# Half-size products for 14 of the 24 column tiles of a linear-attention in-projection, with the residual stream parked in device memory

## The chip, the cores and the metric

The kernel runs on one NeuronCore of a Trainium2 chip. The metric is the device time of one execution in microseconds (us): the median of three runs before the change is 1865.31 us. One further execution was recorded by the hardware profiler; all rows of the profile come from it.

## The reference, cut to what matters

A two-layer decoder over 512 tokens and 16 prepended meta tokens (528 together), width 1024. Each layer is a half-step SwiGLU FFN, a token mixer, and another half-step FFN, each between two RMS norms. Layer 0's mixer is chunked gated linear attention (GLA); the change touches only its in-projection.

```python
def gla_mixer(hn, w_in, w_gate, b_gate, g_head, w_out):      # hn = rmsnorm(h, g[2]), (1, 528, 1024)
    q, k, v, r, lr = jnp.split(hn @ w_in, [512, 1024, 2048, 3072], axis=-1)
    gk = log_sigmoid(lr @ w_gate + b_gate) / 16.0
    ...                                  # 4 heads, key width 128, value width 256, chunks of 64 tokens
    o = o_intra + einsum('bhncd,bhndv->bhncv', q_dec, states)
    o = rmsnorm(o, g_head) * silu(r)     # per head
    return o.reshape(B, L, 1024) @ w_out
h = h + rmsnorm(mix, g[3])
```

`hn @ w_in` has 24 column tiles of 128: 4 of q (tiles 0 to 3, one per head), 4 of k (4 to 7), 8 of v (8 to 15, two per head), 8 of r (16 to 23), and 16 narrow columns lr for the forget gate.

## The kernel before

Everything is kept transposed: features on the 128 partitions, tokens along the free dimension, so that a matmul takes a 128x128 weight tile as the stationary operand and streams tokens. Each float32 operand is split into a high half (rounded to float32r by ScalarE) and a low half (the rest, by VectorE); a product is three matmuls, high x high, low x high, high x low (`mm3s`, and `product` in `Item`).

**Orders.** The order of TensorE's instructions is that of the program text. A small planner in the program, `Flow`, keeps a clock that each matmul moves on; generators (`right_factors`, `core`, `gates`, `gated` and others) yield delays, and their next instructions are put between matmuls when the clock has come so far. The instructions of the other engines and the DMA queues (SP's, POOL's) are put in an order of their own by the compiler's scheduler when the program is built. Each engine then works through its list in order and waits for semaphores.

**Weights.** `units` is the list of weight loads in order of use; `next_w` and `next_pair` take the next one, `prefetch` loads ahead. A plain tile is two raw 128x512 loads and two splits (`split_part`, L268 and L269 of the profile: ScalarE's copy and VectorE's subtraction). A unit that is a list is a pair of tiles for the seven-product scheme (`split_pair`): five raw loads on SP, two accumulating loads on POOL, seven splits (L284, L285) and two additions (L290).

**The seven-product scheme** exists in the FFNs. Two column tiles and the two halves of the contraction (4 k-tiles of 128 each) form a 2x2 block matrix, the two token halves (264 tokens) the other side. `right_factors` scales H by gain and norm factor R into xs, copies H to device memory (`h_kept`) so that its space is free, and makes seven split operands z ("11", "t1", "22", "t2", "21", "t3", "t4"). `Item` with `head`, `body`, `tail` runs the seven products of 12 matmuls in banks a (two), c (two) and d (one), and the next item's head stands before the current one's tail. `Strassen` allots the banks.

**GLA.** `x_first` multiplies the tiles k0, q0, v0, v1; then for each head a generator `core(h)` is spawned, which does scans of the gate, transposes (pv, pm, pk, pt), scores (pa, pb), states (ps, st), outputs (po, pn) and the head's norm (half_go). Meanwhile `x_units` multiplies the next head's four tiles, each over two token groups of 272 and 256 tokens; `evac` multiplies by R out of PSUM. The last eight tiles are r; `gated` applies tanh and the head's output to each of 16 halves and splits the result into og, and `out_proj` follows. A head's core begins when the gates, its tiles and the middle of the previous core are done.

PSUM has eight banks. SBUF holds 42 slots of 128 x 2 x 528 floats and 13 raw slots of 128x512.

## Time and profile before

| | us |
|---|---|
| median of 3 runs (lowest, highest) | 1865.31 (1865.19, 1866.03) |
| the profiled execution | 1864.76 |
| its span, first to last instruction | 1863.0 |
| PE busy (matmul) | 1841.3 |
| DVE busy (VectorE) | 1449.7 |
| ACT busy (ScalarE) | 1145.6 |
| POOL busy (GpSimd) | 375.7 |
| in-projection tiles (`x_l0m`), first to last matmul | 369.7 to 562.1 |

PE is TensorE's matmuls, PEld its weight loads, DVE VectorE, ACT ScalarE, POOL GpSimd, SP the engine that asks for most DMAs; a q behind a name is that engine's queue of DMA issues. A row of groups gives line, engine, operation, output and inputs, count, busy time, the mean of one, then the idle time before them with what ended it. Lines are those of the kernel before. Consecutive instructions of an engine overlap a little, so the pace is read from start to start.

### The profile page before, as it was taken

The page shows a single profiled execution, that of the slowest core. Times are in us where ns is not written, and L with a number is a line of the kernel's source. Part 1 is how long each engine was busy: PE and PEld are TensorE (multiplying, and loading weights), DVE is VectorE, ACT ScalarE, POOL GpSimd, SP SyncE. Part 2 cuts the span into 40 slices and gives each one's busy share as a digit, 9 for nine tenths or more (in the row PEclk, how much of TensorE's full clock was granted, in tenths as well). Part 3 has the DMA queues.
Part 4 walks back from the last instruction along what each step waited for, and adds up shares of the span by engine and source line. Part 5 has one row for each costly group of instructions (what it writes and reads, how often), then busy time and mean ns, then how long its engine had stood idle before and what let it go on. Part 6 is the DMA issues. An engine that isn't in the chain of part 4 may idle for free.

```text
span 1863.0 us, 39130 instructions
## 1 busy us (share of the span) xinstructions
PE 1841.3 (99%) x14743; PEld 1780.2 (96%) x14743; DVE 1449.7 (78%) x2965; ACT 1145.6 (61%) x2677; POOL 375.7 (20%) x535
## 2 busy tenths in 40 slices
PE   9999999999999999999999999999999999999998
PEld 9999999999999999999999899999988898999998
DVE  6887888767664788787888788888767679889884
ACT  5666666654446566666674566666667756666664
POOL 2111113320001411111333111213320141111232
PEclk9999999999999999999999999999999999999999
DMA  7655769421123365576953565769521235557691
GB/s 248 191 147 154 187 149 275 167 69 58 64 62 114 104 180 140 156 182 158 277 200 103 138 162 154 187 152 270 174 74 52 69 103 163 150 158 185 155 292 49
DMA packets 153357, 282.77 MB, mean 152 GB/s; under 512 B 16848, under 2 KB 45392, under 8 KB 153168
## 3 DMA queue, kind: packets, MB, share of 16 engines
q1 hardware_dynamic: 113056, 194.94, 32.5%
q0 software_dynamic: 39680, 84.75, 22.2%
q8 instruction: 115, 1.88, 0.4%
q14 instruction: 74, 0.61, 0.1%
q10 hardware_dynamic: 432, 0.59, 0.1%
HBM read 235.00 MB, written 44.70 MB: 150 GB/s over the span
## 4 chain that ended last, share of the span: by engine, by line
PE 77%; DVE 12%; ACT 6%; issue 3%; DMA 1%; POOL 1%; DVEq 0%; SPq 0%; ACTq 0%; POOLq 0%
PE a L201 22%; PE x L201 17%; PE y L201 16%; PE c L201 11%; PE d L201 5%; DVE raw L290 3%; ACT w_s L284 2%; DVE w L285 2%; DVE w_s L285 1%; DMA raw<-in_w_in 1%; ACT s L1581 1%; ACT w L284 1%; PE po L201 1%; PE o L201 1%; DVE w L269 1%
## 5 line engine op out<-in xcount | busy, mean ns | idle before, releaser
L285 DVE TENSOR_TENSOR w_s<-raw,w_s 128x512 fp32r<-128x512 f32 (+1 forms) x416 | 267.3, 648 | 114.3 <-ACT w_s L284 110.7
L284 ACT ACTIVATE w_s<-raw 128x512 fp32r<-128x512 f32 (+1 forms) x416 | 244.5, 593 | 161.4 <-DVE raw L290 159.9
L285 DVE TENSOR_TENSOR w<-raw,w 128x512 fp32r<-128x512 f32 (+1 forms) x312 | 199.5, 645 | 6.1 <-ACT w L284 4.0
L290 DVE TENSOR_TENSOR raw<-raw,raw 128x512 f32<-128x512 f32 (+1 forms) x304 | 192.1, 632 | 5.2
L344 POOL DMA_DIRECT2D raw<-in_w_in x112 | 103.0, 943 | 444.9 <-DVE w_s L285 72.0
L269 DVE TENSOR_TENSOR w<-raw,w 128x512 fp32r<-128x512 f32 x248 | 166.2, 700 | 33.4 <-ACT w L268 32.1
L284 ACT ACTIVATE w<-raw 128x512 fp32r<-128x512 f32 (+1 forms) x312 | 181.1, 586 | 0.0
L201 PE MATMUL x<-x_l0m,w 128*128 128x272 f32 (+1 forms) x1152 | 152.2, 289 | 0.0
L201 PEld LDWEIGHTS x<-x_l0m,w 128*128 128x128 f32 x1152 | 143.4, 189 | 2.7 <-issue 1.7
L268 ACT ACTIVATE w<-raw 128x512 fp32r<-128x512 f32 x248 | 143.8, 619 | 0.3
L519 POOL TENSOR_TENSOR acc_post<-acc_post,sq_post 128x256 f32<-128x256 f32 (+1 forms) x77 | 61.5, 799 | 361.0 <-ACT sq_post L518 256.7
L201 PE MATMUL y<-hidl0f,w 128*128 128x272 f32 (+1 forms) x960 | 120.4, 286 | 1.2 <-DVE hidl0f L525 1.0
L201 PEld LDWEIGHTS y<-hidl0f,w 128*128 128x128 f32 x960 | 118.1, 188 | 2.2 <-DVE hidl0f L525 1.6
L201 PE MATMUL a<-zl0f_t,w_s 128*128 128x264 f32 x864 | 119.3, 286 | 0.7 <-DVE w_s L285 0.7
L201 PE MATMUL a<-zl1f_t,w_s 128*128 128x256 f32 x864 | 116.1, 283 | 1.2 <-ACT c L1094 0.6
L201 PE MATMUL y<-hidl1f,w 128*128 128x256 f32 (+1 forms) x768 | 115.2, 310 | 0.4 <-DVE hidl1f L525 0.4
L201 PEld LDWEIGHTS y<-hidl1f,w 128*128 128x128 f32 x768 | 104.9, 188 | 9.3 <-DVE hidl1f L525 0.8
L201 PEld LDWEIGHTS a<-zl0f_t,w_s 128*128 128x128 f32 x864 | 110.3, 188 | 2.8 <-DVE w_s L285 1.6
L201 PEld LDWEIGHTS a<-zl1f_t,w_s 128*128 128x128 f32 x864 | 107.1, 188 | 4.1 <-ACT c L1094 1.9
L201 PE MATMUL x<-x_l0f,w 128*128 128x256 f32 (+1 forms) x768 | 98.6, 287 | 1.5 <-DVE w L269 1.1
L201 PEld LDWEIGHTS x<-x_l0f,w 128*128 128x128 f32 x768 | 95.0, 188 | 3.1 <-DVE w L269 1.9
L201 PE MATMUL x<-x_l1f,w 128*128 128x256 f32 (+1 forms) x576 | 93.3, 320 | 2.1 <-ACT x_l1f L547 1.8
(570 smaller groups left out, 4088.3 us busy)
## 6 DMA issues: line engine op xcount, KB each, us to landing
raw<-in_w_in SPq DMA_DIRECT2D x408, 256.0 KB, 4.1
raw<-in_w_in POOLq DMA_DIRECT2D x112, 256.0 KB, 5.1
raw<-in_w_down SPq DMA_DIRECT2D x128, 192.0 KB, 2.3
raw<-in_w_last SPq DMA_DIRECT2D x48, 256.0 KB, 6.3
raw<-in_gla_in SPq DMA_DIRECT2D x48, 256.0 KB, 3.4
kept_y<-dn POOLq DMA_DIRECT2D x16, 528.0 KB, 7.5
raw<-in_w_out SPq DMA_DIRECT2D x32, 256.0 KB, 3.2
kept_y<-dn POOLq DMA_DIRECT2D x16, 512.0 KB, 8.1
```

The source lines that it names most:

```text
L201: inst = pe.matmul(o, lhs, rhs, start=start, stop=stop, skip_group_check=onto)
L268: act.activation(w[:, 0, :m], raw[:, :m], AF.Copy)
L269: dve.tensor_tensor(w[:, 1, :m], raw[:, :m], w[:, 0, :m].bitcast(F32), op=ALU.subtract)
L284: act.activation(w[:, 0, :m], src, AF.Copy)
L285: dve.tensor_tensor(w[:, 1, :m], src, w[:, 0, :m].bitcast(F32), op=ALU.subtract)
L290: dve.tensor_tensor(dst, dst, src, op=ALU.add)
L344: pool.dma_start(r, src, accum_op=ALU.add)
L519: pool.tensor_tensor(sums[0][:, :n], sums[0][:, :n], t[:, :n], op=ALU.add)
L1581: act.activation(s[:, c], s[:, c], AF.Exp, scale=rc[:, c % 2 : c % 2 + 1], bias=nm[:, c : c + 1], accum_out=den[:, c : c + 1],)
```

## The change

Of the 24 tiles, the first ten in order (k0, q0, v0, v1, k1, q1, v2, v3, k2, q2) stay plain. The other fourteen become seven pairs: (v4, v5), (k3, q3), (v6, v7) and four pairs of r. `right_factors` is spawned after `x_first`; it writes H to device memory, and `bring_back_h`, cut out of the FFN, reads it back at the end of the stage. A new `Projected` item evacuates: since the z operands already hold R, five copies on ACT and two additions on DVE per pair replace the multiplications by R. There is one bank c instead of two. `gated` works on 528 tokens at once instead of two halves. Heads 0 and 1 are begun after plain tiles, core 2 after the first pair, core 3 after the third.

```diff
-GLA_ORDER = [4, 0, 8, 9, 5, 1, 10, 11, 6, 2, 12, 13, 7, 3, 14, 15] + list(range(16, 24))
+GLA_ORDER = [4, 0, 8, 9, 5, 1, 10, 11, 6, 2]
+GLA_PAIRS = [(12, 13), (7, 3), (14, 15), (16, 17), (18, 19), (20, 21), (22, 23)]
...
                 units += [a["gla_in"][u] for u in GLA_ORDER]
+                units += [[a["gla_in"][u] for u in pair] for pair in GLA_PAIRS]
...
+    def bring_back_h(kept):
         H.fresh()
         for q in range(KD // 2):
             rows = slice(2 * q, 2 * q + 2)
             pool.dma_start(H[:, rows, kept], h_kept[:, rows, kept])
...
     class Strassen:
-        def __init__(self, z, halves):
+        def __init__(self, z, halves, banks=2):
...
-            self.a, self.c = tiles.a[i], tiles.c[i]
+            self.a, self.c = tiles.a[i], tiles.c[i % len(tiles.c)]
...
+    class Projected(Item):
+        nk = 4
+
+        def __init__(self, tiles, first, second, scale=1.0):
+            super().__init__(tiles)
+            o, n = tiles.o, self.n
+            self.first, self.second = ([t[:, c : c + n] for c in (o, o + n)] for t in (first, second))
+            self.scale = -scale
+
+        def right(self, name, k):
+            return (self.tiles.z[name][k // 2][:, i, k % 2] for i in range(2))
+
+        def body(self):
+            self.product(self.c, "s1", "t1", True)
+            act.activation(self.second[1], self.c, AF.Copy, scale=self.scale)
+            self.product(self.a, "s2", "t2", False)
+            act.activation(self.first[1], self.a, AF.Copy)
+            self.product(self.d, "12", "21", False)
+            act.activation(self.first[0], self.d, AF.Copy)
+            self.product(self.a, "s3", "t3", False)
+            dve.scalar_tensor_tensor(self.second[1], self.a, self.scale, self.second[1], op0=ALU.mult, op1=ALU.add)
+
+        def tail(self):
+            self.product(self.c, "s4", "22", False)
+            dve.tensor_tensor(self.first[1], self.c, self.first[1], op=ALU.add)
+            self.product(self.a, "22", "t4", False)
+            act.activation(self.second[0], self.a, AF.Copy, scale=self.scale)
+            released[0] += 1
...
-            def gated(m, g, p):
-                o, n = g
-                if rg[m] is None:
-                    rg[m] = duo(f"rg{m}")
-                gs, th = (t[:, o : o + n] for t in rg[m])
-                dve.tensor_tensor(gs, p[:, :n], x.rt[:, o : o + n], op=ALU.mult)
+            def gated(m):
+                gs, th = rg[m]
                 act.activation(th, gs, AF.Tanh, scale=0.5)
                 dve.scalar_tensor_tensor(gs, th, 1.0, gs, op0=ALU.add, op1=ALU.mult)
                 yield cores[m // 2 if m < 4 else 3]
...
-                dve.scalar_tensor_tensor(gs, gs, gn, V[:, m, o : o + n], op0=ALU.mult, op1=ALU.mult)
-                split(og[m], gs, g)
+                dve.scalar_tensor_tensor(gs, gs, gn, V[:, m], op0=ALU.mult, op1=ALU.mult)
+                split(og[m], gs, (0, TOK))
...
-            late = []
-            for h in range(HEADS):
-                cores.append(flow.spawn(core(h, [gate] + late + mids[h - 1 : h])))
-                if h + 1 < HEADS:
-                    kk = [("k", h + 1), ("q", h + 1), ("v", 2 * h + 2), ("v", 2 * h + 3)]
-                    late = x_units(x, 4, L0, lambda i, g, p, kk=kk: evac(*kk[i], g, p))
+            n2 = TOK // 2
+            halves, z, plain = [(0, n2), (n2, n2)], {}, Job(None)
+            factors = flow.spawn(right_factors(x, halves, z, plain))
+
+            def begin_core(h, late):
+                cores.append(flow.spawn(core(h, [gate] + late + mids[max(h - 1, 0) : h])))
+
+            begin_core(0, [])
+            kk = [("k", 1), ("q", 1), ("v", 2), ("v", 3)]
+            begin_core(1, x_units(x, 4, L0, lambda i, g, p: evac(*kk[i], g, p)))
+            late = x_units(x, 2, L0, lambda i, g, p: evac("kq"[i], 2, g, p))
+            plain.finish(flow)
+            flow.wait(factors)
+            set_ahead(16, RING)
+            tiles = Strassen(z, halves, 1)
             jobs = []
-            set_ahead(8)
-            x_units(x, KD, L0, lambda i, g, p: jobs.append(flow.spawn(gated(i, g, p))))
-            flow.wait(*jobs[:12])
+            def values(m):
+                return Projected(tiles, V[:, m], V[:, m + 1])
+
+            def keys():
+                qk[3] = duo("qk3")
+                return Projected(tiles, qk[3][1], qk[3][0], 128 ** -0.5)
+
+            def gating(m):
+                rg[m], rg[m + 1] = duo(f"rg{m}"), duo(f"rg{m + 1}")
+                return Projected(tiles, rg[m][0], rg[m + 1][0])
+
+            def finish_gates(m):
+                jobs.extend([flow.spawn(gated(m)), flow.spawn(gated(m + 1))])
+
+            nothing = lambda: None
+            plan = [(lambda: values(4), lambda: begin_core(2, late)), (keys, nothing), (lambda: values(6), lambda: begin_core(3, []))]
+            plan += [(lambda m=m: gating(m), lambda m=m: finish_gates(m)) for m in range(0, KD, 2)]
...
+            cur = begin(0)
+            for i in range(len(plan)):
+                cur.body()
+                nxt = begin(i + 1)
+                cur.tail()
+                plan[i][1]()
+                cur = nxt
+            bring_back_h(slice(0, TOK))
+            flow.wait(*jobs[:6])
             set_ahead(16)
             cap[0] = used[0] + 12
             out_proj(og, L0, L0, True, finish, 5, jobs=jobs, late=2)
```

More of the change, by code (lines that the diff above doesn't have):

```diff
@@ L927, in ffn @@
                 pool.dma_start(Y[:, rows, right], y_right[:, rows, right], accum_op=ALU.add)
+        bring_back_h(kept)
+        set_ahead(32)
+        cap[0] = min(end, len(units))
+        for _ in proj:
+            pass
+    def bring_back_h(kept):
         H.fresh()
@@ L931, in ffn @@
             pool.dma_start(H[:, rows, kept], h_kept[:, rows, kept])
-        set_ahead(32)
-        cap[0] = min(end, len(units))
-        for _ in proj:
-            pass
     def right_factors(x, halves, z, plain):
@@ L987, in trunk_kernel @@
     class Strassen:
-        def __init__(self, z, halves):
+        def __init__(self, z, halves, banks=2):
             self.z, (self.o, self.n) = z, halves[0]
-            self.a, self.c = ([ps(f"{nm}{used[0]}_{i}")[:, : self.n] for i in range(2)] for nm in "ac")
+            self.a, self.c = ([ps(f"{nm}{used[0]}_{i}")[:, : self.n] for i in range(k)] for nm, k in (("a", 2), ("c", banks)))
             self.d = ps(f"d{used[0]}")[:, : self.n]
@@ L1391, in gated @@
                 yield cores[m // 2 if m < 4 else 3]
-                if og[m] is None:
-                    og[m] = pair_tile(f"og{m}")
+                og[m] = pair_tile(f"og{m}")
                 gn = vec[:, V_GN + m % 2 : V_GN + m % 2 + 1]
-                dve.scalar_tensor_tensor(gs, gs, gn, V[:, m, o : o + n], op0=ALU.mult, op1=ALU.mult)
-                split(og[m], gs, g)
+                dve.scalar_tensor_tensor(gs, gs, gn, V[:, m], op0=ALU.mult, op1=ALU.mult)
+                split(og[m], gs, (0, TOK))
             kinds = [("k", 0), ("q", 0), ("v", 0), ("v", 1)]
@@ new lines, in finish_gates, with begin @@
+            def finish_gates(m):
[3 more added lines that the diff above has]
+            plan += [(lambda m=m: gating(m), lambda m=m: finish_gates(m)) for m in range(0, KD, 2)]
+            def begin(i):
+                if i == len(plan):
+                    return None
+                t = plan[i][0]()
+                t.head()
+                return t
```

## The prediction

> **What bounds the kernel now.** I read the page first (spans, slices, the chain that ended last), then the stage the change touches through the views of windows, timeline, groups and waits.

> ```profile
> span 1863.0 us, 39130 instructions
> ...
> PE 1841.3 (99%) x14743; PEld 1780.2 (96%) x14743; DVE 1449.7 (78%) x2965; ACT 1145.6 (61%) x2677; POOL 375.7 (20%) x535
> ...
> PEclk9999999999999999999999999999999999999999
> ...
> PE 77%; DVE 12%; ACT 6%; issue 3%; DMA 1%; POOL 1%; DVEq 0%; SPq 0%; ACTq 0%; POOLq 0%
> ```

> TensorE is busy 99% of the span at full granted clock and carries 77% of the last chain. A matmul saved is worth its pace, as long as VectorE (78%) keeps delivering. The stage itself, beside two windows of the first FFN, where the same seven-product scheme already runs:

> ```profile
> 399.19:562.23 163.04, 163.04 (x1243) 154.46 (x1239) 106.78 (x256) 75.77 (x184) 1.95 (x9) 1.00 0.19 61
> ...
> 100.00:140.00 40.00, 40.00 (x330) 40.00 (x329) 34.61 (x64) 24.94 (x55) 3.44 (x4) 1.00 0.58 142
> ...
> 180.00:220.00 40.00, 38.45 (x308) 37.60 (x307) 33.69 (x59) 25.10 (x57) 9.44 (x11) 1.00 0.83 202
> ```

> Columns are length, then busy time of PE, weight loads, DVE, ACT, POOL, then clock and DMA. The stage has no PE gap, and DVE uses 106.78 of 163.04 us (65%). The FFN products run with DVE at 87% without a gap (100 to 140), or lose 1.55 us (180 to 220).

> **TensorE: what goes.** Fourteen tiles by 8 k-tiles, 2 token groups and 3 products (high and low halves) are 672 matmuls; seven pairs by 7 products, 4 k-tiles and 3 are 588 of 264 columns. Their pace:

> ```profile
> 538.01 24.38 PE L201 MATMUL x<-x_l0m,w 128*128 128x272 f32 x198
> 562.23 13.01 PE L201 MATMUL y<-og,w 128*128 128x272 f32 x105
> ...
> 140.99 1.62 PE L201 MATMUL a<-zl0f_t,w_s 128*128 128x264 f32 x12
> 142.45 1.63 PE L201 MATMUL a<-zl0f,w 128*128 128x264 f32 x12
> ```

> Now (562.23 - 538.01) / 198 = 0.1223 us each; a product of 12 takes 1.46 to 1.47 us, also 0.122. So 84 x 0.1223 = 10.3 us goes. One matmul that zeroes bank d adds 0.1. Net -10.2. The built order shows these counts, and no other stage's PE order moves.

> **VectorE: what is added.** Rates from start to start, on a continuous stretch of the timeline (start, length, what, idle before); the last two rows are groups with busy time and mean:

> ```profile
> 403.52 0.44 DVE L1212 TENSOR_TENSOR qk<-x,R_l0m 128x272 f32<-128x272 f32 x1 [4.61 <-PE x L201]
> ...
> 417.20 2.57 DVE L1253 TENSOR_TENSOR ls<-ls,az 128x528 f32<-128x528 f32 x4 [2.35 <-ACT az L1250]
> ...
> 419.69 1.25 DVE L1265 TENSOR_TENSOR_SCAN b<-resets,ls 128x528 f32<-128x528 f32 x1
> ...
> 422.32 1.27 DVE L269 TENSOR_TENSOR w<-raw,w 128x512 fp32r<-128x512 f32 x2
> ...
> 423.52 0.69 DVE L1283 TENSOR_TENSOR d<-d,qk 128x528 f32<-128x528 f32 x1
> ...
> 449.81 0.41 DVE L1298 TENSOR_TENSOR c<-c,qk 128x256 f32<-128x256 f32 x1
> ...
> L268 ACT ACTIVATE w<-raw 128x512 fp32r<-128x512 f32 x47 | 27.5, 621 | 0.0
> ...
> L1390 DVE SCALAR_TENSOR_TENSOR rg<-rg 128x272 f32<-128x272 f32 x8 | 3.5, 443 | 1.9 <-ACT rg L1389 1.9
> ```

> Four 528-wide take (419.69 - 417.20) = 2.49, so 0.62 each; two 512-wide (423.52 - 422.32) = 1.20, so 0.60; a 264-wide I take as 0.36, the mean of 443 ns for 272 less the overlap of some 0.07 that the other forms show (0.69 against 0.62). Weights: 28 splits become 49, with 14 additions: +35 x 0.60 = 21.0. Factors of the activations: 8 scalings, 14 splits, 8 subtractions: 30 x 0.62 = 18.6. Evacuation: 28 halves become 14 additions: -14 x 0.36 = -5.0. Gating: 48 half-width operations become 24 full ones: 24 x 0.62 - 48 x 0.36 = -2.4. In all +32.2, so 139 us of DVE work in about 163 - 10 = 153: 91%, above the FFN's 87%. ACT gains at most 35 x 0.62 (21 weight and 14 factor splits) + 35 x 0.39 (five evacuations a pair, as 1.56 / 4 of its PSUM reads at 446.38 below) = 35 us, to 111 of 153; it isn't the limit.

> **Where DVE falls behind.** By the built order all 8 scalings, 11 of the 14 factor splits and all 8 subtractions stand in DVE's in-order queue between the arrival of the norm factor R (403.52, the first operation that needs its second half) and the keys of core 1 (L1292, L1298), mixed with core 0's and core 1's own chains; 4 weight splits leave that stretch. PE's order is fixed too: after the last plain tile come core 0's transposes pt, then core 1's pk, then the first product. In before (two windows, then the timeline):

> ```profile
> 403.52:428.02 24.50, 24.50 (x190) 23.90 (x189) 19.81 (x40) 18.22 (x32) 0.00 (x0) 1.00 0.21 66
> ...
> 403.52:449.81 46.29, 46.29 (x350) 43.88 (x348) 35.65 (x81) 28.31 (x60) 0.10 (x1) 1.00 0.22 69
> ...
> 428.48 0.60 PE L213 MATMUL pk<-ident,f 128*128 128x128 f32 x4
> ...
> 445.33 3.90 PE L201 MATMUL x<-x_l0m,w 128*128 128x256 f32 x30
> ...
> 449.07 0.60 PE L213 MATMUL pt<-ident,on 128*128 128x128 f32 x4
> ...
> 442.85 0.17 DVE L463 TENSOR_SCALAR half_go<-sums 128x5 f32<-128x5 f32 x1 [2.86 <-ACT onm L1357]
> ...
> 446.38 1.56 ACT L1364 ACTIVATE on<-po,half_go 128x256 f32<-128x256 f32 x4
> ```

> As a total: DVE's 35.65 us becomes 35.65 + 27 x 0.62 - 4 x 0.60 = 50.0, so it is through at 403.5 + 50.0 = 453.5 at the earliest. PE could want core 1's pk after 15 of those 30 matmuls (3.90 / 30 = 0.13 each) and two pairs of transposes of 0.7 (0.60 in the row of pt, and the small one): 445.33 + 1.9 + 1.4 = 448.6. Bound from below: 4.9 us lost.

> Walked row by row it is lost in three places, each time because a chain's operations stand behind factor operations:
> First, pk of core 0. Ahead of its keys stand 16 factor operations (8 scalings, 6 splits, 2 subtractions) and 3 weight splits less, and one 0.6 us multiply has moved behind: 19.81 + 0.40 + 16 x 0.62 - 3 x 0.60 - 0.60 = 27.7, so 431.2 instead of 428.48: 2.7.
> Second, pt of core 0. The norm chain half_go (ten operations of 0.2) begins 2.7 later, at 445.5, and has three wide weight operations, one multiply and one copy between its steps: 2.0 + 1.8 + 0.6 + 0.3 = 4.7, then ACT's four scalings of 1.56: 451.8. PE is there at 447.2 + 2.7 = 449.9: 1.9.
> Third, pk of core 1: after half_go (450.2) ten more operations worth 4.4 stand up to L1292: 454.6, while PE is there at 451.8 + 1.4 = 453.2: 1.4.
> That makes 6.0. From above: the same with ACT holding the queue's head for another 0.8 us at each place, 8.5. I take +6.3, the walk and a little of the head waits. Nothing hides it: PE has nothing else in its order at these points.

> **After that** DVE has 139 - 50 = 89 us of work in 153 - 49 = 104 of PE's. Two covers are thin. There is one bank c instead of two, so DVE must read a pair's s4 product (the addition of the tail) within the following product, 1.47 us, at each of six turns; and core 2's and 3's chains (half_go, scans) stand among weight splits. Bounds: the FFN's loss of 1.55 in 40 us at the worst, scaled to 104, gives 4.0; its best gives 0; six full turns missed, 6 x 1.47 = 8.8. I take +2.0, nearest the FFN rows.

> **Do the waits cool TensorE?**

> ```profile
> PE x L201 <- ACT x_l1f L547: 1.8, 1, 1.8
> ```

> That is PE's longest wait in before, 1.8 us, and the granted clock is 9 or more tenths in every slice of the page and 1.00 in the windows above. So I add nothing for the clock. [...]

> **Queues that are passed.** POOL now carries 14 accumulating loads. By the built order the first stands between two squares of the FFN's post-norm, the one before the addition at 352.94, and three more stand ahead of or in the chain of the pre-norm factor's second half (yv to dg); SP asks for their plain loads behind its four writes of H. From the timeline, one group, and the DMA issues (median us to landing last):

> ```profile
> 336.68 10.95 SPq L361 DMA_DIRECT2D raw<-in_gla_in  x11
> ...
> 352.94 0.77 POOL L519 TENSOR_TENSOR acc_post<-acc_post,sq_post 128x272 f32<-128x272 f32 x1 [1.48 <-ACT sq_post L518]
> ...
> 393.98 1.88 DVE L269 TENSOR_TENSOR w<-raw,w 128x512 fp32r<-128x512 f32 x3
> ...
> 397.73 0.19 POOL L435 TENSOR_SCALAR yv_l0m<-av_l0m 128x2 int32<-128x2 int32 x1 [3.96 <-ACT av_l0m L434]
> ...
> 400.81 0.61 POOL L479 TENSOR_TENSOR dg_l0m<-ident,yv_l0m 128x256 f32<-128x256 f32 x1
> ...
> 403.32 0.59 PE L201 MATMUL r_l0m<-dg_l0m,ones 128*128 128x256 f32 x2
> ...
> L344 POOL DMA_DIRECT2D raw<-in_w_in x26 | 22.6, 885 | 95.8 <-DVE w_s L285 16.8 <-DVE zl0f L952 14.2 <-DMA raw<-in_w_in 13.3
> ...
> kept_h<-H SPq DMA_DIRECT2D x8, 528.0 KB, 4.9
> ...
> H<-kept_h POOLq DMA_DIRECT2D x8, 528.0 KB, 7.3
> ...
> raw<-in_gla_in SPq DMA_DIRECT2D x48, 256.0 KB, 3.4
> ...
> 604.06 0.44 DVE L599 TENSOR_TENSOR H<-t_l0f,H 128x272 f32<-128x272 f32 x1
> ```

> Each costs POOL 0.9. The first one's load is the last of the eleven that SP asks for up to 347.6 and lands some 3.4 later, 351, in POOL's gap before 352.94: nothing. The last one's load gets its slot from the first of the three splits at 393.98, so from 394.6, and lands 3.4 to 5 us later, about 399, as H's writes are ahead of it: the chain yv to dg, 3.7 us long, then ends near 404 instead of 401.4, while PE has 403.32 - 401.42 = 1.9 of slack: +0.5, bounds 0 and 2.5 (each of two loads 1 us later). H's way back is asked for in the last 20 us of the stage, takes 7.3, and is first needed at 604.06, 42 us after the out-projection begins: nothing. The end of the stage (gates 6 and 7: copy, tanh, two multiplies, split) is some 5.2 us behind three begun units of 54 x 0.1223 = 6.6 us: nothing, by 1.4 us.

> **Sum.** -10.2 + 6.3 + 2.0 + 0.5 = -1.4 us on the profiled execution's 1864.76 (span 1863.0 and 1.76 around it): 1863.4. The median of the runs, 1865.31, lies 0.55 above that execution, so 1863.9. I forecast 1864 us: nearly all of the saved product time goes into waiting for VectorE. Below 0.2% (3.7 us) is about what a measurement of this kernel can tell from no change: "same" is 1861.6 to 1869.0. This case's own range, with the terms' bounds (4.9 to 8.5, 0 to 4.0, 0 to 2.5): 1860.0 to 1870.1; chance 0.55.

> **Rival 1, the queue is no limit.** The factor operations fill DVE's idle time without delaying the keys, as idle time there is (46.29 - 35.65 = 10.6 us in that stretch), so that the front costs 2 us and the turns 1: -10.2 + 3.0 = -7.2, 1858. For it: the FFN at 87% shows 40.00 of 40.00. Against: 16.7 us of factor operations don't fit into 10.6, and less so in order. Chance 0.22.

> **Rival 2, slower: the single bank c.** Each turn's DVE read stands behind a scan or a split, and PE waits a product per turn: 8.8 instead of 2.0, and the two later cores' keys repeat core 1's 1.5 us each: -10.2 + 6.3 + 8.8 + 3.0 + 0.5 = +8.4, 1874. It decides from a delay of 1.47 us of the read at L1161. For it: 91% of DVE. Chance 0.15.

> **Rival 3, waits that cost more than their length.** If matmuls after each of the three front waits ran at half pace for as long as the wait, 6.3 / 2 = 3.1 us come on top: 1867. For it: no row of before shows PE resuming after more than 1.8 us. Against: the clock rows above. Chance 0.08.

> That the change doesn't do what it says is excluded by the built order.

> **How the numbers follow.** The forecast's 0.55 splits 0.15 faster, 0.35 same, 0.05 slower; rival 1 gives 0.22 faster; rival 2 gives 0.02 same and 0.13 slower; rival 3 gives 0.06 same and 0.02 slower. Faster 0.37, same 0.43, slower 0.20. The range for 8 in 10 reaches from rival 1's 1858, less 0.5, to 1871, leaving out most of rival 2.

> **What would show it.** PE waits just before core 0's pk, core 0's pt and core 1's pk, released by DVE f (keys) and ACT on, summing to 4.9 to 8.5 us; DVE above 95% busy from 404 to 454; 588 matmuls on zl0m at 0.122; waits of c on DVE at the turns below 1 us each. Wrong, if those waits are under 3 us, if DVE's 528-wide operations are faster than 0.62, or if a wait of the out-projection on og appears.

## The result, and the profile after

The changed kernel takes 1875.97 us (median; 1873.79 to 1877.66) against 1865.67 for the kernel before: 10.3 us slower, ratio 1.0053, interval 1.0036 to 1.007. The forecast was 1864, with a range that ended at 1871. The profiled execution is the fastest of the four (1873.79 us, mean granted clock 0.996; the others have 0.995 and 0.994), so the account below is of a span 8.7 us longer, and the further 1.6 us of the median lie in executions without a trace.

From the page of the changed kernel: span, TensorE's busy time, the chain that ended last.

```profile
span 1871.7 us, 39133 instructions
...
PE 1839.7 (98%) x14660; PEld 1776.6 (95%) x14660; DVE 1477.6 (79%) x2992; ACT 1174.9 (63%) x2731; POOL 391.4 (21%) x553
...
PE 70%; DVE 15%; ACT 7%; issue 4%; DMA 3%; POOL 1%; DVEq 0%; SPq 0%; ACTq 0%; POOLq 0%
```

The span is 8.7 us longer with fewer matmuls; TensorE's busy time hardly falls (1841.3 to 1839.7), although 84 matmuls have gone: the ones that are left must run slower somewhere. TensorE's waits from 350 to 700 us (who waits, for whom: total, times, longest); in the kernel before this answer holds only r_l0f with 1.5 and y with 0.3:

```profile
PE pk L214 <- DVE f L1326: 3.7, 2, 2.3
PE r_l0m L202 <- POOL dg_l0m L481: 2.8, 1, 2.8
PE a L202 <- ACT rg L1153: 2.6, 1, 2.6
PE r_l0f L202 <- POOL dg_l0f L481: 2.1, 1, 2.1
PE pt L214 <- ACT on L1398: 0.7, 1, 0.7
...
PE c L202 <- DVE V L1161: 0.3, 1, 0.3
```

The stage as a whole and eight stretches of 3.41 us (length; busy time of PE, weight loads, DVE, ACT, POOL; granted clock; DMA). The eight are four pairs, each a stretch with a wait and the one right behind it:

```profile
398.40:568.65 170.25, 160.00 (x1159) 149.26 (x1156) 136.56 (x288) 105.60 (x242) 15.59 (x30) 0.97 0.40 109
...
403.57:406.98 3.41, 1.51 (x11) 1.46 (x11) 0.35 (x2) 0.77 (x2) 1.44 (x6) 1.00 0.41 65
406.98:410.40 3.42, 3.42 (x18) 3.42 (x17) 3.42 (x9) 0.65 (x2) 0.00 (x0) 0.50 0.00 0
430.87:434.28 3.41, 1.55 (x13) 1.34 (x11) 3.41 (x9) 1.86 (x4) 0.00 (x0) 1.00 0.00 0
434.28:437.70 3.42, 2.94 (x25) 2.93 (x26) 3.42 (x8) 0.49 (x1) 0.00 (x0) 1.00 0.00 0
...
560.58:563.99 3.41, 1.36 (x11) 1.36 (x12) 3.18 (x6) 3.41 (x9) 0.00 (x0) 1.00 1.03 407
563.99:567.40 3.41, 3.41 (x18) 3.41 (x17) 2.40 (x5) 0.95 (x2) 0.00 (x0) 0.50 1.05 390
649.33:652.75 3.42, 1.30 (x10) 1.07 (x8) 0.00 (x0) 0.00 (x0) 2.24 (x6) 1.00 0.92 139
652.75:656.16 3.41, 3.41 (x17) 3.35 (x17) 2.68 (x6) 1.55 (x4) 0.00 (x0) 0.50 0.12 20
```

In three of the four pairs TensorE, busy throughout the second stretch, runs it at a granted clock of 0.50, 17 or 18 matmuls instead of some 28 at 0.122 us each. A fourth such stretch is 458.19 to 461.60, behind core 0's pt and core 1's pk: 16 matmuls at 0.50. TensorE's timeline (start, length, what, idle before) gives the prices:

```profile
405.47 0.70 PE L202 MATMUL r_l0m<-dg_l0m,ones 128*128 128x256 f32 x2 [2.81 <-POOL dg_l0m L481]
405.82 5.88 PE L202 MATMUL x<-x_l0m,w 128*128 128x256 f32 x33
411.54 1.94 PE L202 MATMUL z<-lr,wg 128*128 128x272 f32 x8
...
434.76 0.66 PE L214 MATMUL pk<-ident,f 128*128 128x128 f32 x4 [2.34 <-DVE f L1326]
...
458.19 1.12 PE L214 MATMUL pk<-ident,f 128*128 128x128 f32 x4 [1.37 <-DVE f L1326]
...
562.63 1.93 PE L202 MATMUL a<-zl0m_t,w_s 128*128 128x264 f32 x12 [2.56 <-ACT rg L1153]
564.36 2.84 PE L202 MATMUL c<-zl0m,w_s 128*128 128x264 f32 x12
567.00 1.82 PE L202 MATMUL a<-zl0m_t,w 128*128 128x264 f32 x12
568.65 36.75 PE L202 MATMUL y<-og,w 128*128 128x272 f32 x297
```

The last 36 matmuls of the stage take 568.65 - 562.63 = 6.0 us instead of 36 x 0.122 = 4.4: 1.6 lost, near half of that stretch's 3.41 us. The account of the stage, whose out-projection starts at 568.65 instead of 562.23: -10.2 for the matmuls; waits 2.8 + 3.7 + 0.7 + 0.3 + 2.6 = 10.1; three half-clock stretches, some 4.8; transposes pt that follow ScalarE one by one, some 1.4 (the first four take 1.43 instead of 0.60); and -0.8 that the stage was early already at its beginning. That is 5.3 of the 6.4; 1.1 is spread over small rows. Behind the stage the wait of r_l0f is 0.6 longer and is followed by one more half-clock stretch: 2.2 of the remaining 2.3.

### The profile page after: what moved, and what is told of

It is laid out like the page before. It is cut to its first block, busy times and chain, and to the rows that moved or that the text cites. A ratio compares the mean times of both kernels' runs of the same rounds, so it can differ in the third digit from the quotient of the medians.

```text
span 1871.7 us, 39133 instructions
## 1 busy us (share of the span) xinstructions
PE 1839.7 (98%) x14660; PEld 1776.6 (95%) x14660; DVE 1477.6 (79%) x2992; ACT 1174.9 (63%) x2731; POOL 391.4 (21%) x553
## 3 DMA queue, kind: packets, MB, share of 16 engines
q8 instruction: 115, 1.88, 0.4%
## 4 chain that ended last, share of the span: by engine, by line
PE 70%; DVE 15%; ACT 7%; issue 4%; DMA 3%; POOL 1%; DVEq 0%; SPq 0%; ACTq 0%; POOLq 0%
PE a L202 22%; PE y L202 16%; PE c L202 11%; PE x L202 11%; PE d L202 5%; DVE raw L292 3%; ACT w_s L286 3%; DVE w L287 3%; DVE w_s L287 2%; DMA raw<-in_w_in 2%; DVE w L271 1%; ACT w L286 1%; ACT s L1651 1%; PE o L202 1%; PE po L202 1%
## 5 line engine op out<-in xcount | busy, mean ns | idle before, releaser
L287 DVE TENSOR_TENSOR w_s<-raw,w_s 128x512 fp32r<-128x512 f32 (+1 forms) x444 | 286.1, 649 | 117.3 <-ACT w_s L286 113.7
L286 ACT ACTIVATE w_s<-raw 128x512 fp32r<-128x512 f32 (+1 forms) x444 | 262.0, 595 | 164.9 <-DVE raw L292 163.4
L287 DVE TENSOR_TENSOR w<-raw,w 128x512 fp32r<-128x512 f32 (+1 forms) x333 | 213.6, 647 | 12.3 <-ACT w L286 10.0
L292 DVE TENSOR_TENSOR raw<-raw,raw 128x512 f32<-128x512 f32 (+1 forms) x318 | 201.5, 634 | 5.2
L286 ACT ACTIVATE w<-raw 128x512 fp32r<-128x512 f32 (+1 forms) x333 | 194.1, 588 | 0.0
L271 DVE TENSOR_TENSOR w<-raw,w 128x512 fp32r<-128x512 f32 x220 | 147.7, 702 | 25.2 <-ACT w L270 23.9
L270 ACT ACTIVATE w<-raw 128x512 fp32r<-128x512 f32 x220 | 127.3, 619 | 0.3 <-DMA raw<-in_w_in 0.2
L202 PEld LDWEIGHTS x<-x_l1f,w 128*128 128x128 f32 x576 | 81.8, 188 | 10.7 <-ACT x_l1f L549 2.0
L202 PE MATMUL x<-x_l0m,w 128*128 128x272 f32 (+1 forms) x480 | 64.9, 293 | 0.0
## 6 DMA issues: line engine op xcount, KB each, us to landing
raw<-in_w_in SPq DMA_DIRECT2D x408, 256.0 KB, 4.1
raw<-in_w_in POOLq DMA_DIRECT2D x112, 256.0 KB, 5.0
raw<-in_gla_in SPq DMA_DIRECT2D x55, 256.0 KB, 3.4
raw<-in_w_last SPq DMA_DIRECT2D x48, 256.0 KB, 5.9
kept_y<-dn POOLq DMA_DIRECT2D x16, 528.0 KB, 7.8
raw<-in_w_out SPq DMA_DIRECT2D x32, 256.0 KB, 3.0
```

Of the source, the lines that this page charges most:

```text
L202: inst = pe.matmul(o, lhs, rhs, start=start, stop=stop, skip_group_check=onto)
L270: act.activation(w[:, 0, :m], raw[:, :m], AF.Copy)
L271: dve.tensor_tensor(w[:, 1, :m], raw[:, :m], w[:, 0, :m].bitcast(F32), op=ALU.subtract)
L286: act.activation(w[:, 0, :m], src, AF.Copy)
L287: dve.tensor_tensor(w[:, 1, :m], src, w[:, 0, :m].bitcast(F32), op=ALU.subtract)
L292: dve.tensor_tensor(dst, dst, src, op=ALU.add)
```

## The experiments

Times are differences of medians from the kernel before in the same comparison; the changed kernel stands at +10.3.

**The POOL queue.** In the changed kernel's POOL timeline an accumulating load waits 4.8 us for its plain load and holds the norm chain behind it; another 0.9 us load stands inside the chain:

```profile
399.90 0.88 POOL L346 DMA_DIRECT2D raw<-in_gla_in  x1 [4.77 <-DMA raw<-in_gla_in]
...
401.10 0.88 POOL L346 DMA_DIRECT2D raw<-in_gla_in  x1
...
404.81 0.61 POOL L481 TENSOR_TENSOR dg_l0m<-ident,yv_l0m 128x256 f32<-128x256 f32 x1
```

```diff
-                for r, src in ((s1, a22), (s3, a11)):
-                    pool.dma_start(r, src, accum_op=ALU.add)
+        # in split_pair, for the first two pairs, once the factor's chain is queued:
+            for r, src in sums:
+                after(norm["dg"], pool.dma_start(r, src, accum_op=ALU.add))
```

> The changed kernel with one edit: the accumulating loads of the first two pairs stand behind the pre-norm factor's second half in POOL's queue instead of ahead of and inside it. My account of the lost time (10.3 us above the kernel before by the medians): 2.8 us are TensorE's wait for that factor, and some 1.7 us more are the 3.4 us of half granted clock that follow it, so this kernel should stand about 4.5 us below the changed one, near +6 us (ratio 1.003), with no wait of r_l0m on dg and clock 1.00 from 400 to 430. Rival A (VectorE's backlog sets the end of the front anyway): the 2.8 us come back as longer waits before core 0's keys and core 1's keys, and the time stays near +10. Rival B (the wait was 2.8 us and nothing follows from the clock): near +7.5.

+6.7 us (1.0032, 1.002 to 1.0044): 3.6 less than the changed kernel. The wait of r_l0m is gone, and the half clock behind it; 0.9 of the 2.8 came back as a longer wait before core 0's pk (3.3 instead of 2.3), and in the profiled execution the stretch behind that wait (432.68 to 436.09) now runs at half clock, 19 matmuls at 0.50. So its span is only 1.4 us shorter (1870.3).

**The end of the stage.** ScalarE's timeline: its in-order queue has the split og of gates 4 and 5, which waits 2.73 us for VectorE, ahead of the two copies that empty the banks of the last pair:

```profile
559.66 1.32 ACT L526 ACTIVATE og<-rg 128x528 fp32r<-128x528 f32 x2 [2.73 <-DVE rg L1424]
560.89 0.37 ACT L1151 ACTIVATE rg<-c 128x264 f32<-128x264 f32 x1
...
562.20 0.38 ACT L1153 ACTIVATE rg<-a 128x264 f32<-128x264 f32 x1
```

```diff
                 yield cores[m // 2 if m < 4 else 3]
+                if 4 <= m < 6:
+                    yield copied        # finished behind the last pair's body()
```

> The changed kernel with one edit: the last multiplication and split of gates 4 and 5 wait until the last pair's first four products are copied out, so that ScalarE's queue no longer holds that pair's copies of c and a behind the split of og. My account: TensorE's wait of 2.6 us before the last pair's s3 product goes, and with it 1.7 us of half clock: 4.3 us below the changed kernel, near +6 us. Rival (the tail of the stage is bound by VectorE's backlog): the wait moves to the out-projection, which then waits for og by 2 us or more, and the time stays near +10.

+6.4 us (1.0033, 1.002 to 1.0046), 3.9 less. The wait is gone, and no wait of y on og took its place.

**Both queues.**

> The changed kernel with the edits of both queue experiments: the accumulating loads behind the norm factor on POOL, and gates 4 and 5 behind the last pair's copies on ScalarE. If the two places are independent their gains add: -3.8 and -4.1 us (medians against the changed kernel), so near +2.4 us on the kernel before. Rival (they share one backlog of VectorE): the second edit adds 1 us or less, near +5.5.

+1.6 us (1.0008, 0.9999 to 1.0016). The gains add (3.6 + 3.9 against 8.7, within the intervals). So these two queues cost 8.7 us, half-clock stretches included.

**The clock.** Filler in front of two norm factors:

```diff
         r = ps(f"r_{name}")
+        if name in ("l0m_272", "l0f1_272"):    # 10 and 8 times
+            pe.matmul(r[:, :P], ones, ones, start=True, stop=True)
```

> The changed kernel with 10 and 8 dummy matmuls in front of the pre-norm factor's second half in this stage and in the next FFN: TensorE waits as long as before for the factor but isn't idle. If an idle stretch halves the clock of the next 3.41 us window, both half-clock windows (407 to 410, 653 to 656) go and the time falls by 2 x 1.7 = 3.4 us, to near +7. Rival (matmuls run slow there because of contention with loads or VectorE, or as a restart after any wait): nothing gained, near +10, and the slow rows remain.

+9.7 us (1.005, 1.0037 to 1.0063), 0.6 less, inside the uncertainty. TensorE's timeline with the filler:

```profile
403.36 2.39 PE L491 MATMUL r_l0m<-ones 128*128 128x128 f32 x20
405.59 0.68 PE L202 MATMUL r_l0m<-dg_l0m,ones 128*128 128x256 f32 x2
405.92 4.35 PE L202 MATMUL x<-x_l0m,w 128*128 128x256 f32 x33
410.11 1.94 PE L202 MATMUL z<-lr,wg 128*128 128x272 f32 x8
...
434.25 0.70 PE L214 MATMUL pk<-ident,f 128*128 128x128 f32 x4 [3.26 <-DVE f L1329]
```

The factor arrives as before, but the 33 matmuls behind it take 4.19 us (405.92 to 410.11) instead of 5.72, and the half-clock stretch is gone: it does come from the idle time. In the FFN, where the factor comes 9.7 us after the second st_l0f with and without filler, the way from that st_l0f to the first product of hidl0f is 27.0 us instead of 28.6. In the stage, though, nothing was won: core 0's pk waits 3.26 instead of 2.34, and the stretch behind it (434.73 to 438.15, after one with 2.93 us idle) now runs at half clock, 18 matmuls at 0.50, which it did not in the changed kernel. VectorE delivers these keys 28.7 us after the factor (29.3 in the changed kernel), whether TensorE is fast or slow until then. My 3.4 us were too many because one of the two slow stretches lay ahead of that wait and came back as waiting.

The same in the kernel before, with nothing of the change:

```diff
+        if name == "l0f1_272":
+            for _ in range(8):
+                pool.tensor_scalar(yy, yy, 1.0, None, op0=ALU.mult)
```

> The kernel before, with nothing of the change, and 8 dummy operations of 0.28 us on POOL inside the chain that gives r_l0f: TensorE's wait there should be 1.5 + 2.2 = 3.7 us. If an idle stretch halves the clock of the next 3.41 us window, the time rises by 2.2 + 1.7 = 3.9 us (ratio 1.0021) and the trace shows a granted clock of 0.50 for 3.4 us behind the wait. Rival (the half clock of the changed kernel comes from its products, its loads or VectorE's load, not from the pause): +2.2 us, and clock 1.00.

The pause came out longer than meant: with a load of 0.9 us that slipped in between, the eight operations took 3.8 us, and the chain began 0.4 later. TensorE waits 6.0 us for r_l0f instead of 1.5; the stretches:

```profile
643.40:649.40 6.00, 0.06 (x1) 0.00 (x0) 0.00 (x0) 0.00 (x0) 4.41 (x16) 0.72 0.47 79
649.40:652.70 3.30, 3.25 (x13) 3.08 (x14) 1.58 (x4) 0.89 (x3) 0.00 (x0) 0.50 0.00 0
```

+5.3 us (1.003, 1.0019 to 1.0042): 4.5 of pause, and half clock until 652.7. The time's interval reaches from 3.5 to 7.8 us and does not tell 4.5 from 4.5 + 1.6; the clock and the 13 matmuls in 3.3 us do.

**The front.** Keys later in TensorE's order:

```diff
-                yield STATE_KEYS + (0 if h else BEHIND)
+                yield STATE_KEYS + (0 if h else BEHIND) + {0: 5.0, 1: 4.0}.get(h, 0.0)
```

> The changed kernel with one edit to TensorE's order: the transposes pk of core 0 stand 45 plain matmuls (5.5 us) later and those of core 1 behind the first products of the first pair instead of before them. My account: the front is set by when VectorE gets to these keys, so TensorE waited (2.3 and 1.4 us before the two pk, 0.7 and some 1.0 of slow transposes at pt, 1.7 of half clock) only because its fixed order had nothing else there; with other work in front 4 to 6 us go, to near +5 us on the kernel before. Rival (VectorE is the bound of the whole front, whatever TensorE's order): the wait moves to the first products of the pair, which need VectorE's factors and weight splits too, and the time stays near +10.

+9.1 us (1.0052, 1.0039 to 1.0065). Both waits of pk are gone, and one of 4.4 us has come; from TensorE's waits and ScalarE's timeline:

```profile
PE a L202 <- ACT d L1074: 4.4, 1, 4.4
...
458.14 0.63 ACT L286 ACTIVATE w_s<-raw 128x512 fp32r<-128x512 f32 x1 [1.35 <-DVE half_go L471]
```

The first pair's copy d frees the bank that the next product needs. Its product is done at 453.77, but the copy starts at 459.20: ScalarE's queue has seven operations of the cores, the factors and the weights ahead of it, one of them the split above, which waits 1.35 us for VectorE. With both queues mended the result is alike:

> The changed kernel with all three edits: accumulating loads behind the norm factor, gates 4 and 5 behind the last pair's copies, and the transposes pk of cores 0 and 1 later in TensorE's order. If the three places are independent, -3.8, -4.1 and about -5 us add to the changed kernel's +10.3: near -2.5 us, the first version below the kernel before. Rival (VectorE bounds the front): near +2.

+1.5 us (1.0008, 0.9999 to 1.0017), no better than without the keys' edit.

Fewer factor operations (half of the factors' splits are left out, and each second factor takes the first one's tiles, so the results are not those of the reference):

```diff
             for c, b in enumerate(src):
+                if c and x.name == "l0m":
+                    z[name].append(z[name][0])
+                    continue
```

> The changed kernel with 7 of the 14 high and low splits of the activation factors left out (each second one uses the first one's tiles, so the products of the pairs are not those of the reference): 7 operations fewer on VectorE and on ScalarE in the front, nothing else moved on TensorE. If VectorE's queue sets the keys' time, 3 splits fewer stand ahead of core 0's pk (-1.9 us of its wait of 2.3) and 7 ahead of core 1's (-4.3 us, all of the 1.4, 0.7 and 1.0 there): 4 to 6 us below the changed kernel, near +5. Rival (the planner's place of these transposes, or ScalarE's chain on, sets it): the waits stay within 0.5 us of what they were.

+7.3 us (1.0036, 1.0022 to 1.005), 3.0 less, below what I expected, and not by the way I expected: from the factor to core 0's pk it is 28.7 us instead of 29.3, because the scheduler put two subtractions more ahead of the keys, where three splits had gone. For core 0's keys the run doesn't decide its question. Core 1's keys come no earlier either (TensorE goes on 51.4 us after VectorE's first operation with the factor, 51.6 in the changed kernel), though five factor splits fewer and one weight split more stand ahead of them: VectorE idles 2.86 us there before half_go, waiting for ScalarE's onm, a step of core 0's chain. What the trace shows for the 3.0 us is the clock: one half-clock stretch in the stage and none behind r_l0f, instead of three and one.

The front in another order: factor operations behind core 0's keys, each product waiting for its own factor, and shorter delays for these operations in the planner.

```diff
         for job in x.rjob:
             yield job
+        if keyed is not None:
+            yield keyed                  # finished behind core 0's keys
...
+            flow.wait(self.tiles.made[name])      # Projected.right
...
-            flow.wait(factors)
+            flow.wait(made["11"])
```

> The changed kernel with one place edited, the front of the stage: the activation factors are queued on VectorE after core 0's keys instead of ahead of them, each product of the pairs waits for its own factor instead of for all of them, and the planner reckons 0.5 and 0.7 us for a scaling and a factor operation instead of 0.8 and 1.1. By the built order core 0's chain is then as in the kernel before, the ten operations of its norm stand nearly together, and core 0's pt and core 1's pk lie between products. My account: VectorE's order, not its amount of work, cost the front its waits (2.3 + 0.7 + 1.4 us, 1.0 of slow transposes, 1.7 of half clock), so 4 to 7 us go, to near +5 on the kernel before. Rival (VectorE's amount of work bounds the front, as the run with the keys later suggests): the wait appears before the first products, 4 us or more, and the time stays near +10.

+13.2 us (1.0068, 1.0055 to 1.008), above the changed kernel (whose interval, 1.0036 to 1.007, overlaps). In its trace the load on POOL holds r_l0m for 3.6 us, and six stretches of the stage run at half clock, 0.50 each. With both queues mended:

> The changed kernel with the two queue edits (accumulating loads behind the norm factor; gates 4 and 5 behind the last pair's copies), which stood at +1.6 us on the kernel before, and the edit of the front. If the front's loss was one of order: 4 to 8 us less, -3 to -6 us on the kernel before (ratio 0.997 to 0.998). Rival (amount of work): +1 to +2, as with the keys later.

+2.5 us (1.0013, 1.0004 to 1.0022), no gain over the two queues alone. TensorE's waits from 404 to 525 and the stretches there:

```profile
PE pt L214 <- ACT on L1422: 1.8, 1, 1.8
PE a L202 <- DVE zl0m_t L976: 1.7, 1, 1.7
PE pk L214 <- DVE f L1348: 1.6, 1, 1.6
...
452.03:455.44 3.41, 0.89 (x6) 0.67 (x6) 3.41 (x9) 1.84 (x5) 0.00 (x0) 1.00 0.06 20
455.44:458.85 3.41, 2.74 (x12) 2.74 (x13) 3.41 (x7) 3.35 (x8) 0.00 (x0) 0.50 0.42 133
458.85:462.27 3.42, 3.42 (x21) 3.04 (x20) 2.91 (x7) 1.29 (x3) 1.60 (x2) 0.50 0.72 171
```

Core 0's waits are gone; the sum, with 0.7 at the single bank c, is 5.8 us, as it was 5.6 with the queues alone. Here the order decided where TensorE waits in the front, hardly how long.

The same with the next FFN's first accumulating loads behind that FFN's factor (e11), and then one more edit each: six pairs instead of seven (e13), core 1's chain later (e14), the factors' subtractions on POOL (e15), core 0's and 1's norm on POOL (e16). Six pairs had been tried on the changed kernel alone as well (e3).

> As the kernel with the front and both queues edited, and the accumulating loads of the next FFN's first pair stand behind that FFN's norm factor on POOL as well (two of them stood inside its chain, 2.1 us of wait of r_l0f against 1.5 in the kernel before). 0.6 us less wait, and a half-clock window of 1.7 us in about half of the executions: 0.6 to 2.3 us less, about -5 to -7 on the kernel before.

> The changed kernel with tiles 12 and 13 multiplied plainly, so six pairs instead of seven, and the six begin 11.7 us of product time later. By the count of products it loses 12 matmuls, 1.5 us. My account: the waits before core 1's keys and pt (0.7 and 1.4 us), the slow transposes (1.0) and one half-clock window (1.7) at 454 to 462 go, and the accumulating loads move in POOL's queue as well, so it is 3 to 7 us below the changed kernel. Rival (the pairs themselves, by VectorE's work per pair, cost the time wherever they begin): 1.5 us above the changed kernel less one pair's VectorE work, about the same as it.

> The kernel with all four edits (+0 us on the kernel before), and tiles 12 and 13 multiplied plainly, six pairs instead of seven: 11.7 us more of TensorE's work that needs no factor, at a price of 12 matmuls, 1.5 us. What is left in the front of the kernel with four edits is 5.1 us of waits (1.6 before core 1's keys, 1.7 for the factor t2, 1.8 at core 1's pt) and two half-clock windows (3.4 to 3.7). If that is VectorE's amount of work, 46 us to be done before TensorE has as much of its own, most of the 8.8 us goes: -5 to -7 us (ratio 0.9965). Rival (it is the order again): the waits stay, +1.5 us.

> The kernel with all four edits, and core 1's chain (scans, decays, keys, norm) begun 8 us after core 0's values are out, behind the first products of the first pair, on all engines. If VectorE's amount of work in the front is the bound, taking some 8 us of core 1's operations out of it takes away the wait before core 1's keys and the wait for t2 with their half-clock windows: -4 to -7 us on the kernel before. Rival (the wait moves to the first products, whose splits and factors are then late): 0 to +2 us.

> The kernel with all four edits, and the 8 subtractions of the activation factors on POOL, which stands idle there, instead of VectorE: 5 us less on VectorE. If VectorE's amount of work is the bound, the two waits at core 1's keys and at t2 (1.6 + 1.7 us) shrink to below 1 us with one half-clock window less: -3 to -5 us on the kernel before. Rival (the chain of subtractions, longer on POOL, is then the late one): the wait for t2 or the next factor grows to over 3 us, +1 to +4 us.

> The kernel with all four edits, and the norm of cores 0 and 1 (ten operations of some 0.15 us, between which VectorE's queue has put longer ones) on POOL as twelve. If the order among these operations delays core 1's pt (1.8 us), that wait goes and some of VectorE's time with it: -2 to -3 us on the kernel before. Rival (amount of work of the longer operations): 0.

| kernel | us, ratio (interval) | TensorE's waits 408 to 525 | half-clock stretches in the stage |
|---|---|---|---|
| e11, four edits | -0.3, 0.9999 (0.999 to 1.0008) | 5.8 | 3 |
| e3, six pairs only | +12.4, 1.0067 (1.0054 to 1.0079) | 7.8 | 4 |
| e13, four and six pairs | +1.6, 1.0005 (0.9996 to 1.0014) | 5.5 | 3 |
| e14, four and core 1 later | +1.6, 1.0009 (1.0 to 1.0018) | 7.4 | 3 |
| e15, four and POOL subtractions | -4.1, 0.9977 (0.9968 to 0.9985) | 5.4 | 0 |
| e16, four and POOL norm | +1.7, 1.0012 (1.0003 to 1.0021) | 7.7 | 2 |

e11 stands 2.7 us below e10, a little more than the 0.6 to 2.3 written for that step, but not at the time expected. e3, e13, e14 and e16 went their rivals' way or further. e15 met its time, but not for the reason given: it hardly waits less. Its waits from 404 to 525:

```profile
PE pk L214 <- DVE f L1350: 1.4, 1, 1.4
PE po L202 <- DVE st L1398: 1.3, 1, 1.3
PE a L202 <- DVE w L298: 1.0, 1, 1.0
PE a L202 <- DVE zl0m_t L978: 0.9, 2, 0.7
PE pt L214 <- ACT on L1424: 0.8, 1, 0.8
```

5.4 us like e11's 5.8, but in six pieces of at most 1.4 us, spread from 448 to 478, and none cost a half-clock stretch, where e11 has three. The stage's out-projection starts at 560.17, the earliest of all kernels, 2.0 us before that of the kernel before.

What the edits would give the kernel before, and the subtractions alone:

> The kernel before with one of the four edits, the only one that does not need the change: the accumulating loads of the next FFN's first pair behind that FFN's norm factor on POOL. One load stands ahead of that chain there (0.9 us), and TensorE waits 1.5 us for r_l0f. So 0.9 us less, and the kernel with all edits and the subtractions on POOL still stands about 3 us below it. Rival (that kernel's lead of 4 us comes from this queue in the main): 1.5 us or more less.

> The changed kernel with one edit: the 8 subtractions of the activation factors on POOL instead of VectorE, 2 of them ahead of core 0's keys and all 8 ahead of core 1's; TensorE's order is the same. If VectorE's amount of work bounds the front in the changed kernel too: 1.2 us less wait before core 0's pk (2.3 to 3.3 in the runs so far), most of the 0.7 and 1.4 us of core 0's pt and core 1's pk gone, and the half clock behind them: 3 to 5 us below the changed kernel, near +6. Rival (in that order the first product waits for the chain of subtractions on POOL): no gain, near +10, with a wait of a on a factor.

The kernel before with the one edit it can use: -3.2 us (0.9984, 0.9975 to 0.9993); its wait of r_l0f, 1.5 us in the profile, is gone. The other 1.7 may be half clock: in this comparison the kernel before has a mean granted clock below 1.000 in 12 of 15 executions, with the edit in 3 of 11; the profiled execution is not one of the 12, so no trace shows the stretch. The 3.2 are most of e15's 4.1, so the rival holds: mended in every place that I found, the change is worth 0.9 us over a kernel without it, less than the intervals can tell. The subtractions alone: +12.4 us (1.0065, 1.0053 to 1.0078). There POOL works while VectorE has core 0's scans; POOL's and VectorE's timelines of that kernel:

```profile
427.82 2.15 POOL L965 TENSOR_TENSOR xsl0m<-xsl0m,xsl0m 128x528 f32<-128x528 f32 x1
...
426.48 2.38 DVE L1299 TENSOR_TENSOR_SCAN b<-resets,ls 128x528 f32<-128x528 f32 x1
428.78 2.31 DVE L1300 TENSOR_TENSOR_SCAN b<-resets,ls 128x528 f32<-128x528 f32 x1
```

and of the changed kernel:

```profile
425.00 1.25 DVE L1299 TENSOR_TENSOR_SCAN b<-resets,ls 128x528 f32<-128x528 f32 x1
426.17 1.23 DVE L1300 TENSOR_TENSOR_SCAN b<-resets,ls 128x528 f32<-128x528 f32 x1
```

The scans take nearly twice as long, so moving work to POOL gave VectorE nothing there, and pk waits 5.2 us. (r_l0m waits 3.7 instead of 2.8 as well, for the same load on POOL.) In e15, too, VectorE's time did not fall: with the eight subtractions on POOL its 278 operations of the stage take 135.05 us, where e10's 286 take 134.18 (one split of zl0m_t takes 1.47, the median 0.70), so e15 does not settle whether VectorE's amount of work is the bound.

## Why the prediction was wrong, point by point

- **TensorE, -10.2: right.** 588 matmuls on zl0m; a product of 12 takes 1.47 us, 0.1225 each.
- **VectorE, +32.2 to 139 us: right.** 136.56 in the stage, against 106.78: +29.8.
- **Front, 2.7 + 1.9 + 1.4, taken as 6.3: right in place, nearly in size.** 2.3, 0.7 and 1.4 us, and 0.9 of slow transposes at pt. VectorE was reckoned through 50.0 us after the factor; core 1's keys let TensorE go at 458.19, 51.6 after VectorE's first operation with it (406.62). Of my signs, the three waits sum to 4.4, just below the 4.9 asked for, and VectorE is busy 92% from 404 to 454 (45.94 of 50.00 us); from 406.62 to 458.19 it is 97% (49.78 of 51.57). What bounds the front stays open. Sums of waits that hardly change with the order (5.3 to 5.8 in e9, e10, e11 and e15) fit VectorE's amount of work. But the changed kernel has 4.7, and e14, e16, e3 and e18 have 7.4 to 8.7; and e13, with 11.7 us more of TensorE's work that needs no factor, still waits 5.5, which speaks against it, as do core 1's keys in e8, where VectorE idled. No run took work away cleanly: e8 was refilled ahead of core 0's keys, and in e15 and e18 VectorE's other operations got longer.
- **Later turns, +2.0: over-sized.** 0.3 at the single bank c, and a slow pt of some 0.5. Rival 2 comes closest in time (1874) by a mechanism that did not occur. Rival 1's 1 us for the turns is near, its 2 us for the front is not.
- **POOL's queue, +0.5 (0 to 2.5): right mechanism, mis-sized.** The chain ended at 405.42 instead of my 404: a second load of 0.9 us stood inside it, and TensorE was there at 402.66. The wait was 2.8, above my upper bound.
- **End of the stage, 0: the step that failed.** I weighed gates 6 and 7 against TensorE's remaining products and did not ask what stands ahead of the last pair's copies in ScalarE's queue: the split of gates 4 and 5. It cost 2.6 us, and 3.9 with what followed (e2). The sign that I had set for this place, a wait of the out-projection on og, did not appear.
- **The clock, 0: the other step that failed.** I added nothing for the clock behind waits of 2.7, 1.9 and 1.4 us, on rows of before whose longest wait was 1.8 us; its trace shows no half clock. The half-clock stretches cost some 4.8 us in the stage and 1.6 behind it, the largest miss of the sum. Rival 3 had the effect, but as half of each wait's length, and only in the front; what the rows show is some 1.6 us for a stretch of 3.41 us, and in e12 a wait of 6.0 us has no more of TensorE's work at half clock behind it (3.30 us) than one of 2.8 us has in the changed kernel (3.41).
- **The rest, unchanged: nearly.** Two accumulating loads slipped into the chain of r_l0f: 0.6 us, and the stretch counted above.

So the forecast's -1.4 became +8.7 on the span: 6.4 for the clock, 2.6 for ScalarE's queue, 2.9 for POOL's in both places, less some 2 that the front and the turns were over-sized. The median's further 1.6 is in no trace.

## What to carry to other kernels

When work is added to engines beside a full TensorE, walk the in-order queue of every engine that empties a PSUM bank or feeds a norm, and ask what stands ahead of that instruction and what it waits for: 8.7 of the loss sat in two such places and went with two edits. Count waits not only by their sum but by their size: e11, with 5.8 us in three pieces of 1.6 to 1.8 and one of 0.7, stands 3.8 us above e15, with 5.4 us in pieces of 1.4 and less. By the traces three half-clock stretches against none account for it; that e15's edit did nothing else is not shown. And before a change's repaired version is praised, give the kernel before the repairs it can use.

## What the hardware showed

```profile
404.54:407.96 3.42, 1.65 (x12) 1.60 (x13) 0.50 (x2) 0.92 (x3) 1.39 (x5) 1.00 0.44 69
407.96:411.37 3.41, 3.41 (x29) 3.33 (x28) 3.41 (x8) 0.51 (x1) 0.00 (x0) 1.00 0.02 5
```

Where transposes surround the wait, less idle time by the profile was enough (1.45 us from 454.77 to 458.19, though 1.47 from 453.82 to 457.23 in e15 was not); why isn't settled. Nor is why a slow stretch with no wait to speak of is sometimes followed by another: 455.44 to 458.85 in e10 idled 0.67 us, and the next one stayed at half clock.

**VectorE beside POOL.** Two scans that took 1.25 and 1.23 us in the changed kernel, with POOL idle, took 2.38 and 2.31 in e18 beside POOL's subtractions. Why they are longer isn't shown.
